# Hybrid convolution and gated linear attention block: the transposes of a token tile's scaled outputs one half-unit step later in the recurrence

## Chip, cores and metric

The kernel runs on one core of one Trainium2 chip. The metric is the device time of one execution in microseconds (us), the median of repeated runs.

## What is computed

One layer on x of shape 512 tokens x 2048. `h = rms_norm(x)`; one projection `h @ w_in` gives the inputs of two branches; their outputs side by side go through `w_out`, are added to x and normalised again. All is float32. The branch that matters here is the gated linear attention, with 4 heads, chunks of 64 tokens, and a state of 128 x 256 for each head:

```python
u = jnp.einsum('bnchk,bnchv->bnhkv', k_dec, vc)      # one update for each chunk and head
def step(state, inp):
    d, du = inp
    state = d[..., None] * state + du
    return state, state
_, s_all = lax.scan(step, init, (decay, u))
o = jnp.einsum('bnchk,bnhkv->bnchv', qc, s_all)      # every frame reads the state at its chunk's end
o = o * lax.rsqrt(jnp.mean(o * o, axis=-1, keepdims=True) + EPS) * norm_g
y_gla = o * jax.nn.silu(r)
```

The other branch is a gated short convolution over 1024 channels.

## The kernel before, in words

Tokens are held in 4 token tiles of 128 (`TT`), each of two chunks. Matrix products are made from float32r pairs: each operand is split into a rounded part (`hi`, a cast on ScalarE) and a rest (`lo`, a subtraction on VectorE), and three products hi*hi, lo*hi and hi*lo are summed in PSUM (`mm3`, lines 157 to 159).

The kernel goes through these stages. First the token-major projections (keys, values and the gate's input; tile names `tm`). Then the feature-major projections `ft`: 12 units (`ft_unit`), four for q and eight for r (`r_block`), each of 48 matmuls of 128x512 in two halves of 24. Then four Strassen-like units `st_unit` for the convolution's inputs (lines 591 to 645, tiles `pa` to `pf`, `st`, `sq`), and the output projection with its final norm (`po`, and a fifth `st_unit`).

The recurrence has no stage of its own. It is the generator `gla_steps` (line 436), and `ft_unit` calls `step()` after each half of its 24 matmuls, so the generator advances by one yield with every half unit. Step k therefore stands in the program right after half unit k, counted from 1; half units 1 to 8 belong to q, 9 to 24 to r. Where a unit ends between two steps, its tail stands between them too: for r, a multiplication on VectorE (line 493), a Silu on ScalarE (line 494) and a store to DRAM (line 495).

- Steps 1 to 6: gate, decays, and the split of token tile 0's keys and values.
- `pair_state(tt)`, steps 7, 10, 13 and 16: 24 matmuls `u` into four PSUM tiles (line 363), the state updates on VectorE (line 375), and each new state's split (`sp_hi`, `sp_lo`, lines 151 and 152).
- `chunk_splits(tt + 1)`, steps 8, 11 and 14: the split of the next tile's keys and values.
- `pair_out(tt)`, steps 9, 12, 15 and 18: 16 matmuls of q with the states into four PSUM tiles (lines 391 and 392), then the halves added (lines 394 and 395), then `out_norm`: four squares with their sums on ScalarE (line 408), a small operation on VectorE (413), a power on GpSimd (415), and four scalings of `o` by the result on ScalarE (420).
- `out_transpose(tt)`, steps 10, 13, 16 and 19 for tiles 0 to 3: eight TensorE transposes of the scaled `o` into two PSUM tiles `tp` (line 429), and eight ScalarE copies of 128x128 with the gain into `oT` (line 432). `oT` is first read much later, by `gated_rows` (line 478).

The PSUM tiles `u`, `o` and `tp` all come from one pool, `aux`, of four banks; the `ft` sums have four banks of their own. Temporaries of 128x512 come from one pool of 44 buffers (`t2`). The framework gives every engine a fixed order of instructions when the program is built: mainly the program's order, with later instructions put ahead where it expects earlier ones not to be ready. On the chip each engine works through its queue in that order.

```python
    def out_transpose(tt, o):
        for pr in range(2):
            tp = aux(f"tp{tt}_{pr}")
            for i in range(4):
                nc.tensor.transpose(out=tp[:, isl], in_=o[pr][:, isl], identity=ident)
            for i in range(4):
                nc.scalar.activation(oT[4 * pr + i][...], tp[...], AF.Copy, scale=g_v[...])
```

Of the kernel before, what the change touches and what calls it, by code (L numbers as in the profile page):

```python
# [49 lines left out]
def hybrid_block(ctx: ExitStack, tc: tile.TileContext, xT, x, params, w_tm, w_ft, w_st, w_up, b_gate, w_out, final_g, out):  # L50
# [11 lines left out]
    def t2(name):  # L62
        return k2.tile([P, S], F32, tag="k2", name=name)
# [7 lines left out]
    def aux(name):  # L71
        return ps_aux.tile([P, S], F32, tag="aux", name=name)
# [75 lines left out]
    def split_small(t, name):  # L148
        hi = t2r(f"{name}_hi")
        lo = t2r(f"{name}_lo")  # L150
        nc.scalar.copy(out=hi, in_=t)
        nc.vector.tensor_sub(out=lo, in0=t, in1=hi.bitcast(F32))
        return hi, lo
# [148 lines left out]
    def gate_transpose():  # L302
        gT = aux("gT")
        for tt in range(TT):
            nc.tensor.transpose(out=gT[0:GST, tt * P : (tt + 1) * P], in_=gst[:, tt, :], identity=ident)
        ga = t2r("ga")
        nc.vector.tensor_copy(out=ga[0:GST, :], in_=gT[0:GST, :])
        return ga

    def gate(tt, ga):  # L310
        z = aux(f"z{tt}")
        nc.tensor.matmul(z, lhsT=ga[0:GST, tt * P : (tt + 1) * P], rhs=wst, start=True, stop=True)
        e = t2(f"e{tt}")
        nc.scalar.activation(e, z, AF.Abs)
        nc.scalar.activation(e, e, AF.Exp, scale=-1.0)
        nc.scalar.activation(e, e, AF.Ln, bias=1.0)
        nc.vector.scalar_tensor_tensor(out=e, in0=z, scalar=0.0, in1=e, op0=ALU.min, op1=ALU.subtract)
        return split_small(e, f"gl{tt}")

    def gate_decay(tt, gl):  # L320
        sfx = aux(f"sfx{tt}")
        nc.tensor.matmul(sfx, lhsT=tri, rhs=gl[0], start=True, stop=False)
        nc.tensor.matmul(sfx, lhsT=tri, rhs=gl[1], start=False, stop=True)
        e = t2(f"ke{tt}")
        nc.scalar.activation(e, sfx, AF.Exp)
        for j in range(2):
            row = (j + 1) * CHUNK - 1
            nc.scalar.dma_start(out=dec8[2 * tt + j : 2 * tt + j + 1, :], in_=e[row : row + 1, :])
        nc.vector.scalar_tensor_tensor(
            out=kv[tt][0], in0=e, scalar=tail, in1=kv[tt][0], op0=ALU.max, op1=ALU.mult  # L330
        )

    def chunk_decays():
        dp = aux("dp")
        for hh in range(HEADS):
            nc.tensor.transpose(
                out=dp[:, hh * NCH : (hh + 1) * NCH], in_=dec8[0:NCH, hh * HK : (hh + 1) * HK],
                identity=ident[0:NCH, 0:NCH],
            )
        nc.vector.tensor_copy(out=decay, in_=dp[:, 0 : HEADS * NCH].rearrange("p (h c) -> p h c", c=NCH))  # L340
# [8 lines left out]
    def chunk_splits(tt):  # L349
        kv_split[tt] = [split_small(kv[tt][j], f"kv{tt}_{j}") for j in range(3)]  # L350

    def pair_state(tt):
        kp = kv_split[tt][0]
        for pr in range(2):
            vp = kv_split[tt][1 + pr]
            us = [aux(f"u{2 * tt + j}_{pr}") for j in range(2)]
            for i in range(2):
                hh = 2 * pr + i
                ksl, vsl = slice(hh * HK, (hh + 1) * HK), slice(i * HV, (i + 1) * HV)
                for k, (a, b) in enumerate(((0, 0), (0, 1), (1, 0))):  # L360
                    for j in range(2):
                        rows = slice(j * CHUNK, (j + 1) * CHUNK)
                        nc.tensor.matmul(
                            us[j][:, vsl], lhsT=kp[a][rows, ksl], rhs=vp[b][rows, vsl], start=k == 0, stop=k == 2
                        )
            for j in range(2):
                n = 2 * tt + j
                st = t2(f"s{n}_{pr}")
                if state[pr] is None:
                    nc.vector.tensor_copy(out=st, in_=us[j])  # L370
                else:
                    for i in range(2):
                        hh = 2 * pr + i
                        vsl = slice(i * HV, (i + 1) * HV)
                        nc.vector.scalar_tensor_tensor(
                            out=st[:, vsl], in0=state[pr][:, vsl], scalar=decay[:, hh, n : n + 1],
                            in1=us[j][:, vsl], op0=ALU.mult, op1=ALU.add,
                        )
                state[pr] = st
                split_state[n, pr] = split_small(st, f"sp{n}_{pr}")  # L380
# [16 lines left out]
    def pair_out(tt):  # L397
        o = [t2(f"o{tt}_{pr}") for pr in range(2)]
        for j in range(2):
            chunk_out(2 * tt + j, o)  # L400
        out_norm(tt, o)
        return o
# [19 lines left out]
    def out_transpose(tt, o):  # L422
        if not oT:
            oT.extend(t2(f"oT{b}") for b in range(8))
# [3 lines that stand above are left out]
                isl = slice(i * P, (i + 1) * P)  # L428
                nc.tensor.transpose(out=tp[:, isl], in_=o[pr][:, isl], identity=ident)
            for i in range(4):  # L430
                blk = 4 * pr + i
                nc.scalar.activation(
                    oT[blk][:, tt * P : (tt + 1) * P], tp[:, i * P : (i + 1) * P], AF.Copy, scale=g_v[:, blk : blk + 1]
                )

    def gla_steps():
        ga = gate_transpose()
        yield
        gl = []
        for tt in range(TT):  # L440
            gl.append(gate(tt, ga))
            if tt % 2:
                yield
        for tt in range(TT):
            gate_decay(tt, gl[tt])
            if tt % 2:
                yield
        chunk_decays()
        chunk_splits(0)
        yield  # L450
        done = None
        for tt in range(TT):
            pair_state(tt)
            if done is not None:
                out_transpose(tt - 1, done)
            yield
            if tt + 1 < TT:
                chunk_splits(tt + 1)
            yield
            done = pair_out(tt)  # L460
            yield
        out_transpose(TT - 1, done)

    steps = gla_steps()

    def step():
# [569 lines left out]
```

## Time and profile before

| | us |
|---|---|
| median of 3 runs | 791.43 |
| lowest and highest run | 790.61, 791.45 |
| the profiled execution, its own time | 790.9 |
| its span, first to last instruction | 788.9 |
| TensorE busy in the span | 772.4 |
| VectorE busy | 564.7 |
| ScalarE busy | 379.9 |
| GpSimd busy | 31.2 |

The profile is of one execution. Its instructions span 788.9 us, and its own time, measured as the runs are, is 790.9 us, 0.5 us under the median. Engine names in rows are PE (TensorE matmuls), PEld (its weight loads), DVE (VectorE), ACT (ScalarE), POOL (GpSimd) and SP (the queue of DMA issues). A tile is named without its number. `out<-in` says what an instruction writes and reads. In a timeline the columns are start, duration, engine, line, operation, tiles, shape and count; a bracket gives the idle time of the engine before it and what ended it. A matmul's recorded duration overlaps the next one's, so distances are taken from start to start.

### The profile page before, as it was taken

The numbers are of one execution on the slowest core, as the hardware profiler recorded it, in microseconds if no ns is written. First come the engines' busy times: TensorE is split into PE (matmuls) and PEld (weight loads), VectorE is DVE, ScalarE is ACT, GpSimd is POOL, SyncE is SP. The second block draws the span as 40 slices with busy tenths as digits, with TensorE's granted clock in tenths as the row PEclk, the third lists the DMA queues.
The fourth block names the chain that finished last, engine by engine and source line by source line (L and its number), as shares of the span: only waits on it lengthen the run. The fifth ranks groups of instructions, "written<-read, shape, count | busy, mean of one in ns | idle before, by whom it ended". The sixth has DMA issues, their size and how long they took to land. (4 is left out here: it accounts for less than half of the span.)

```text
span 788.9 us, 10098 instructions
## 1 busy us (share of the span) xinstructions
PE 772.4 (98%) x3752; PEld 663.4 (84%) x3752; DVE 564.7 (72%) x711; ACT 379.9 (48%) x574; POOL 31.2 (4%) x38
## 2 busy tenths in 40 slices
PE   9999999999999999999999999999999999999995
PEld 8999999887777878888788888888888888888885
DVE  7533242466666529998998699968987997997913
ACT  6552122364688646644544444445436344643504
POOL 1000000000000000000000000000000000003601
PEclk9999999999999999999999999999999999999998
DMA  9973334222132327877875656654655359668006
GB/s 317 324 257 88 108 121 133 88 95 76 64 107 67 103 82 260 288 219 263 297 235 187 209 179 201 211 191 164 226 186 170 127 182 364 200 195 293 24 1 213
DMA packets 48933, 140.39 MB, mean 178 GB/s; under 512 B 5827, under 2 KB 7875, under 8 KB 48885
## 3 DMA queue, kind: packets, MB, share of 16 engines
q1 hardware_dynamic: 48628, 139.74, 53.3%
q8 instruction: 29, 0.48, 0.2%
q14 instruction: 20, 0.16, 0.1%
q10 hardware_dynamic: 256, 0.02, 0.0%
HBM read 130.29 MB, written 9.44 MB: 177 GB/s over the span
## 5 line engine op out<-in xcount | busy, mean ns | idle before, releaser
L116 ACT CAST hi_sq_t<-raw_sq 128x1024 fp32r<-128x1024 f32 x80 | 84.2, 1055 | 118.5 <-PE pa L591 24.9
L117 DVE TENSOR_TENSOR lo_sq_t<-raw_sq,hi_sq_t 128x1024 fp32r<-128x1024 f32 x80 | 98.6, 1236 | 22.0 <-ACT hi_sq_t L116 21.8
L645 DVE TENSOR_TENSOR raw_sq<-raw_sq,raw_sq 128x1024 f32<-128x1024 f32 x80 | 97.0, 1219 | 5.6 <-DMA raw_sq<-in_w_st 4.7
L116 ACT CAST hi_st<-raw_st 128x1024 fp32r<-128x1024 f32 x60 | 63.2, 1054 | 68.4 <-PE pa L591 20.6
L117 DVE TENSOR_TENSOR lo_st<-raw_st,hi_st 128x1024 fp32r<-128x1024 f32 x60 | 72.1, 1220 | 13.6 <-ACT hi_st L116 13.6
L157 PE MATMUL ft<-hhi,hi_ft 128*128 128x512 f32 x192 | 75.8, 395 | 0.0
L158 PE MATMUL ft<-hlo,hi_ft 128*128 128x512 f32 x192 | 75.4, 392 | 0.0
L159 PE MATMUL ft<-hhi,lo_ft 128*128 128x512 f32 x192 | 75.2, 392 | 0.0
L117 DVE TENSOR_TENSOR lo_tm<-raw_tm,hi_tm 128x776 fp32r<-128x776 f32 x24 | 23.2, 966 | 59.1 <-ACT hi_tm L116 55.8
L262 PE MATMUL tm<-hi_tm,hhi 128*128 128x388 f32 x256 | 55.8, 339 | 0.9 <-DVE hi_tm L143 0.9
L262 PE MATMUL tm<-hi_tm,hlo 128*128 128x388 f32 x256 | 55.6, 339 | 0.0
L262 PE MATMUL tm<-lo_tm,hhi 128*128 128x388 f32 x256 | 55.4, 338 | 0.0
L116 ACT CAST hi_tm<-raw_tm 128x776 fp32r<-128x776 f32 x24 | 20.2, 842 | 68.7 <-PE tm L262 65.8
L117 DVE TENSOR_TENSOR lo_ft<-raw_ft,hi_ft 128x1024 fp32r<-128x1024 f32 x24 | 29.4, 1224 | 25.4 <-ACT hi_ft L116 25.4
L262 PEld LDWEIGHTS tm<-hi_tm,hhi 128*128 128x128 f32 x256 | 46.1, 188 | 1.1 <-ACT hhi L169 1.1
L262 PEld LDWEIGHTS tm<-lo_tm,hhi 128*128 128x128 f32 x256 | 46.0, 188 | 0.0
L262 PEld LDWEIGHTS tm<-hi_tm,hlo 128*128 128x128 f32 x256 | 45.9, 188 | 0.0
L157 PEld LDWEIGHTS ft<-hhi,hi_ft 128*128 128x128 f32 x192 | 36.1, 188 | 7.6 <-issue 0.2
L159 PEld LDWEIGHTS ft<-hhi,lo_ft 128*128 128x128 f32 x192 | 36.1, 188 | 7.6
L158 PEld LDWEIGHTS ft<-hlo,hi_ft 128*128 128x128 f32 x192 | 36.1, 188 | 7.0
L116 ACT CAST hi_ft<-raw_ft 128x1024 fp32r<-128x1024 f32 x24 | 25.2, 1050 | 31.7 <-PE ft L158 18.7
L157 PE MATMUL po<-hi_wo,yh 128*128 128x512 f32 (+1 forms) x104 | 39.6, 381 | 0.0
(279 smaller groups left out, 1642.7 us busy)
## 6 DMA issues: line engine op xcount, KB each, us to landing
raw_sq<-in_w_st SPq DMA_DIRECT2D x64, 512.0 KB, 4.1
raw_st<-in_w_st SPq DMA_DIRECT2D x48, 512.0 KB, 3.9
raw_ft<-in_w_ft SPq DMA_DIRECT2D x24, 512.0 KB, 3.5
raw_tm<-in_w_tm SPq DMA_DIRECT2D x24, 388.0 KB, 3.4
raw_sq<-in_w_out SPq DMA_DIRECT2D x16, 512.0 KB, 4.1
raw_wo<-in_w_out SPq DMA_DIRECT2D x13, 512.0 KB, 3.9
raw_st<-in_w_out SPq DMA_DIRECT2D x12, 512.0 KB, 7.5
rawx<-in_xT SPq DMA_DIRECT2D x16, 256.0 KB, 4.8
```

The costliest lines, as they stand in the source:

```text
L116: nc.scalar.copy(out=hi, in_=full)
L117: nc.vector.tensor_sub(out=lo, in0=full, in1=hi.bitcast(F32))
L157: nc.tensor.matmul(ps, lhsT=ah, rhs=bh, start=first, stop=False)
L158: nc.tensor.matmul(ps, lhsT=ah, rhs=bl, start=False, stop=False)
L159: nc.tensor.matmul(ps, lhsT=al, rhs=bh, start=False, stop=last)
L262: nc.tensor.matmul(pst[tt][:, 0:TMC], lhsT=a[:, tt * P : (tt + 1) * P], rhs=w, start=kt == 0 and k == 0, stop=kt == KT - 1 and k == 2,)
L645: nc.vector.tensor_tensor(out=dst, in0=x0, in1=x1, op=op)
```

## The change

In the loop over token tiles, `out_transpose(tt - 1, done)` stands after the yield that follows `pair_state(tt)` and no longer ahead of it, so it runs at the start of the step that also holds `chunk_splits(tt + 1)`: tiles 0, 1 and 2 in steps 11, 14 and 17 and no longer 10, 13 and 16. One more yield puts tile 3's from step 19 into step 20. No instruction is added or taken away, no size changes, and nothing of the moved part issues a DMA.

```diff
@@ -451,14 +451,15 @@
         done = None
         for tt in range(TT):
             pair_state(tt)
+            yield
             if done is not None:
                 out_transpose(tt - 1, done)
-            yield
             if tt + 1 < TT:
                 chunk_splits(tt + 1)
             yield
             done = pair_out(tt)
             yield
+        yield
         out_transpose(TT - 1, done)
 
     steps = gla_steps()
```

## Rows read from the trace of the kernel before

**Rows 1.** The profile page: its head.
```profile
span 788.9 us, 10098 instructions
```

**Rows 2.** Waits of TensorE, whole run: waiter <- releaser, us in total, times, longest.
```profile
PE tp L429 <- ACT o L420: 4.5, 4, 1.9
PE tp L429 <- ACT oT L432: 1.4, 1, 1.4
...
PE pa L591 <- DVE lo_st L117: 0.7, 1, 0.7
```

**Rows 3.** Windows: stretch, its length, busy us of each engine, clock, DMA, GB/s.
```profile
200.00:282.00 82.00, 76.03 (x420) 62.54 (x419) 49.62 (x82) 63.91 (x146) 4.04 (x4) 1.00 0.28 87
320.00:360.00 40.00, 40.00 (x178) 33.10 (x178) 40.00 (x41) 20.86 (x25) 0.00 (x0) 1.00 0.75 235
388.00:789.00 401.00, 392.98 (x1809) 327.27 (x1808) 328.09 (x362) 180.30 (x227) 23.62 (x16) 0.99 0.57 189
```

**Rows 4.** Timeline of TensorE: start, duration; a bare half unit, sixteen transposes.
```profile
281.98 0.39 PE L157 MATMUL ft<-hhi,hi_ft 128*128 128x512 f32 x1
...
287.42 0.39 PE L157 MATMUL ft<-hhi,hi_ft 128*128 128x512 f32 x1
...
624.20 0.60 PE L730 MATMUL tu<-ident,c 128*128 128x128 f32 x4
...
625.86 0.48 PE L157 MATMUL po<-hi_wo,yh 128*128 128x512 f32 x1
```

**Rows 5.** Timeline of TensorE around the transposes of token tile 0.
```profile
207.20 0.50 PE L157 MATMUL ft<-hhi,hi_ft 128*128 128x512 f32 x1
...
210.08 0.44 PE L429 MATMUL tp<-ident,o 128*128 128x128 f32 x2 [1.92 <-ACT o L420]
...
215.86 0.39 PE L157 MATMUL ft<-hhi,hi_ft 128*128 128x512 f32 x1
...
221.30 0.28 PE L391 MATMUL o<-sp_hi,qs 128*128 128x256 f32 x1
```

**Rows 6.** Timeline of TensorE around the transposes of token tile 1.
```profile
230.39 0.50 PE L157 MATMUL ft<-hhi,hi_ft 128*128 128x512 f32 x1
...
238.88 0.39 PE L157 MATMUL ft<-hhi,hi_ft 128*128 128x512 f32 x1
```

**Rows 7.** Timeline of TensorE around the transposes of token tile 2.
```profile
253.19 0.28 PE L363 MATMUL u<-kv_hi,kv_lo 64*128 64x256 f32 x2
...
257.26 0.66 PE L429 MATMUL tp<-ident,o 128*128 128x128 f32 x4 [1.43 <-ACT oT L432]
...
261.86 0.39 PE L157 MATMUL ft<-hhi,hi_ft 128*128 128x512 f32 x1
```

**Rows 8.** Timeline of TensorE: the half unit with the transposes of token tile 3 begins.
```profile
274.68 0.39 PE L157 MATMUL ft<-hhi,hi_ft 128*128 128x512 f32 x1
```

**Rows 9.** Timeline of ScalarE: start, duration, idle time before it and its releaser.
```profile
218.25 2.17 ACT L432 ACTIVATE oT<-tp,par 128x128 f32<-128x128 f32 x8
...
220.94 1.28 ACT L494 ACT_TABLE_LOAD   x1
...
228.66 1.05 ACT L116 CAST hi_ft<-raw_ft 128x1024 fp32r<-128x1024 f32 x1 [0.50 <-PE ft L158]
...
234.49 1.71 ACT L420 ACTIVATE o<-o,ro 128x256 f32<-128x256 f32 x4 [0.90 <-POOL ro L415]
...
252.88 1.71 ACT L420 ACTIVATE o<-o,ro 128x256 f32<-128x256 f32 x4 [1.32 <-POOL ro L415]
```

**Rows 10.** Timeline of VectorE: state updates, then the handover to the quarter sums.
```profile
212.38 0.87 DVE L375 SCALAR_TENSOR_TENSOR s<-s,decay,u 128x256 f32<-128x256 f32 x2
...
257.30 0.87 DVE L375 SCALAR_TENSOR_TENSOR s<-s,decay,u 128x256 f32<-128x256 f32 x2
...
293.06 0.69 DVE L493 TENSOR_TENSOR r<-ft,rB 128x512 f32<-128x512 f32 x1 [8.80 <-PE ft L159]
...
298.96 0.69 DVE L525 TENSOR_TENSOR qs<-raw_qx,raw_qx 128x512 f32<-128x512 f32 x1
```

## The prediction, made before the changed kernel ran

> **What bounds the kernel now.** I read the page's head for the span [rows 1], then TensorE's own waits over the whole run [rows 2], the windows [rows 3], and last the timelines of each stretch with a wait [rows 4 to 10]. Outside one stretch TensorE works without a pause: it is busy 40.00 of 40 us in one later window and 392.98 of 401 in the last, which holds the program's tail [rows 3]. From 200 to 282 us it is busy only 76.03 of 82 [rows 3], and the missing 6.0 us are the waits of the transposes `tp`: 4.5 us in four waits for the scaling of `o` on ScalarE, 1.4 us in one wait for the copies into `oT`, that is, for a PSUM bank [rows 2]. The rest of the run has one wait of 0.7 us for VectorE worth naming [rows 2]. So TensorE's queue sets the end, and the change moves just those instructions that make it stand still.
>
> **What each stand costs.** A half unit with nothing in it takes 5.44 us (281.98 to 287.42), and sixteen transposes in a row take 1.66 (624.20 to 625.86), so eight take about 0.85 with the return to other matmuls [rows 4]. What a half unit with transposes takes beyond 5.44 + 0.85 = 6.29 us is lost:
> - tile 0: 207.20 to 215.86 is 8.66, so 2.3 lost [rows 5];
> - tile 1: 230.39 to 238.88 is 8.49, so 2.2 lost [rows 6];
> - tile 2: its last `u` starts at 253.19, the transposes could follow 0.2 later at 253.4, and the next half unit starts at 261.86: 8.46, so 2.15 lost [rows 7];
> - tile 3: 274.68 [rows 8] to 281.98 [rows 4] is 7.30, so 0.95 lost.
>
> Together 7.6 us. It is more than the 6.0 us recorded as waits, because a matmul's recorded end lies after the point at which the next could start, and because the transposes come in lots of two and four between other matmuls.
>
> **The change part by part.** Nothing is added or removed. All 32 transposes and 32 copies move one step later, past one half unit of 24 matmuls, 5.44 us of TensorE; SP's and GpSimd's queues are not touched, since the moved code issues neither a DMA nor a GpSimd instruction. What it costs is what is late next, tile by tile.
>
> Tile 0. The transposes would be reached at 207.20 + 5.44 = 212.64, two and a half microseconds after their data came (210.08) [rows 5]. The second lot needs a second bank, which the state update on VectorE gives back at 212.38 + 0.87 = 213.25 [rows 10]; TensorE is there at 213.1. I count 0.15 lost, so 2.15 gained.
>
> Tile 1. TensorE would start the half unit at 230.39 - 2.15 = 228.24 and be at the transposes at 233.7. The four scalings run on ScalarE from 234.49 to 236.20 [rows 9], and ScalarE is busy 63.91 of the 82 us [rows 3], without a pause of note ahead of them but two: 0.50 us in which a cast waits for TensorE, and 0.90 us for the power on GpSimd [rows 9]. The first goes when TensorE is earlier, the second stays. So the last transpose can't end before about 235.9 to 236.4, where 234.55 would be free of waits: 1.3 to 1.8 lost. I take 1.5, so 0.7 gained. If tile 0 gains less, this wait shrinks by as much: ScalarE sets where TensorE stands after tile 1, at about 2.85 us ahead of now.
>
> Tile 2. TensorE arrives at 253.4 - 2.85 + 5.44 = 256.0. The scalings, 252.88 to 254.59 [rows 9], are over even if they come no earlier. The second bank is given back by the update at 257.30 + 0.87 = 258.17 now [rows 10]; its chain runs over ScalarE, earlier by at least the 0.5 us above and at most by TensorE's 2.85, so between 255.3 and 257.7, against a need at 256.5. Between no wait and 1.2 I take 0.5, so 1.65 gained. Should the bank still be the one that the first lot's copies free, the present wait of 1.43 [rows 7] is the bound.
>
> Tile 3. The transposes come 3.9 us of matmuls later than they stand now, and the wait there is at most what was lost, 0.95. I take it as gone.
>
> The copies. ScalarE makes tile 0's from 218.25, eight microseconds after the first transposes, as their place in its queue is behind the state's casts [rows 9]. So they needn't move when the transposes come at 212.6. They end at 220.42 and free the two banks that the third and fourth `o` products want; TensorE would reach the first of them at 221.30 - 2.15 = 219.15 [rows 5] and the third and fourth 1 to 1.4 us later, at 220.1 and 220.6. That fits by 0.2 us at the worst. What could be late is the unit tail that the copies now pass in the program: its Silu with a table load of 1.28 us [rows 9]. If it comes first, about 1.9 us are lost here, but TensorE then waits that much less at tile 1, so the sum is the same but for a few tenths. For later tiles I count 0.15 for such waits.
>
> The sum: 2.15 + 0.7 + 1.65 + 0.95 - 0.15 = 5.3 us. The profiled execution took 790.9 us in all, of which 788.9 are its span [rows 1]: 790.9 - 5.3 = 785.6. It was 0.5 us under the median of the runs, so I predict 786.1 us.
>
> Whether it lasts to the end: VectorE waits 8.80 us for TensorE before the quarter sums begin at 293 [rows 10], so all that follows is timed from TensorE and moves with it; nothing between there and the end is tied to a fixed time.
>
> A rule that speaks against the change: a gap that repeats on the busy engine, says the Trainium skill in "Perfetto Trace Analysis", section "Optimization Strategy", can mean that there is not enough SBUF or PSUM for the next tile. By it the sum would be about zero, since the banks would be held longer. The trace bears it out for 1.4 of the 6.0 us alone [rows 2].
>
> **The rivals.** *All waits go.* ScalarE's order changes too, and the scalings of tile 1 come before its other work. The whole 7.6 us are gained: 783.8. For it: ScalarE does work there that is not urgent, such as the scaling of later inputs. Against: nothing in the change moves that work.
>
> *The wait moves to the banks.* The copies go one half unit later on ScalarE as well: tile 0's would end at 220.42 + 5.44 = 225.9, and the fourth `o` product, due at 220.6, waits 5.3 us. TensorE is then at tile 1's transposes at 233.7 + 5.3 = 239.0 and done at 239.85, 1.0 behind now, with 1.65 + 0.95 still to gain: 1.6 gained in all, 789.8. Against: the copies already stand late in ScalarE's queue and needn't move.
>
> *Nothing moves, or nothing lasts.* Queue orders are not quite the program's: tile 0's transposes stand three matmuls inside the half unit and not ahead of it [rows 5]. They might keep their places; or what is gained is waited for again where VectorE is at 40.00 of 40 us [rows 3] and TensorE already waits 0.7 us for it [rows 2]. Time 791.4. Against: VectorE's wait of 8.80 us before that stretch [rows 10].
>
> *Slower.* VectorE has no reserve between 320 and 360 us [rows 3]. If the new order pushes the quarter sums, now begun while TensorE is still in the r units, into that stretch, TensorE pays for each at the product that waits 0.7 us now. A quarter's work takes VectorE 5.2 us (293.75 to 298.96 [rows 10]); two of them cost 10.4, so 786.1 + 10.4 = 796.5. It decides from about 6.9 us pushed, 5.3 plus the bound of no change. Against: the sums are tied to half units 21 to 24, behind everything moved.
>
> **How the numbers follow.** A measurement of this kernel can tell about 0.2%, 1.6 us, from no change. Chances: forecast 0.66, all waits go 0.09, banks 0.11, nothing 0.08, slower 0.06. The forecast alone runs from 785.1 (1.3 us lost at tile 1 and nothing elsewhere) to 788.3 (1.8 at tile 1, 1.43 at tile 2, and as much again above the count at another bank). Adding the first two rivals gives 783.8 to 789.8, which leaves out 0.14 and a margin. The bank rival lies on the bound of 0.2%, so half of it counts as faster: faster 0.66 + 0.09 + 0.05 = 0.80, same 0.08 + 0.06 = 0.14, slower 0.06.
>
> **What would show it.** In the changed profile the transposes stand behind a whole half unit of `ft` matmuls; TensorE's waits for the scaling of `o` fall from 4.5 us to 1 to 2, all at tile 1; the half units with transposes take 6.3 to 6.5 us for tiles 0 and 3, near 8 for tile 1, near 7 for tile 2; the first matmul of `pa`, right after the last `ft`, starts about 5 us earlier, and the end with it. A wait of `o` for the `oT` copies, or of `pa` for `lo_st` grown from 0.7 us, would prove me wrong, and so would transposes found at their old places.

## The result, and the profile after

The changed kernel takes **786.03 us** (median of 6 runs, 785.87 to 788.13); the kernel before, run beside it, 791.25 (6 runs, 790.61 to 792.25). The ratio is 0.9938, 95% interval 0.9925 to 0.9951. The profiled execution took 785.95 us, 783.6 of them its span. From line 463 on the changed kernel's line numbers are one higher, and an experiment's are shifted by the lines that it adds. One run of the kernel before, beside e9_state to e11_state_before, took 1343.82 us at a mean clock of 0.634 and is left out of its median there.

The head and first part of the profile page of the changed kernel, answering [rows 1]:

```profile
span 783.6 us, 10104 instructions
...
PE 773.7 (99%) x3752; PEld 664.8 (85%) x3752; DVE 563.7 (72%) x711; ACT 379.9 (48%) x574; POOL 31.6 (4%) x38
```

TensorE's waits over the whole run, answering [rows 2] (waiter <- releaser, total, times, longest):

```profile
PE warm L86 <- POOL ones L83: 1.1, 1, 1.1
PE o L391 <- ACT oT L432: 0.7, 1, 0.7
```

The first is the warm-up at the start. Of the 4.5 us for the scaling of `o`, the 1.4 us for a bank and the 0.7 us of `pa` for `lo_st`, nothing is left; one wait of `o` for the `oT` copies is new. The windows, answering [rows 3], the later two moved by about 5 us:

```profile
200.00:282.00 82.00, 81.28 (x440) 67.39 (x439) 50.93 (x84) 65.45 (x148) 4.04 (x4) 1.00 0.29 90
315.00:355.00 40.00, 40.00 (x178) 33.14 (x177) 40.00 (x40) 21.31 (x25) 0.00 (x0) 1.00 0.75 235
383.00:784.00 401.00, 392.65 (x1808) 326.96 (x1806) 327.07 (x362) 180.24 (x227) 24.02 (x16) 0.99 0.58 189
```

TensorE is busy 81.28 of 82 us where it was at 76.03. The timeline of TensorE in the changed kernel, answering [rows 5 to 8]; matmuls between the shown ones are left out:

```profile
207.09 0.50 PE L157 MATMUL ft<-hhi,hi_ft 128*128 128x512 f32 x1
...
212.66 1.24 PE L429 MATMUL tp<-ident,o 128*128 128x128 f32 x8
213.66 0.48 PE L157 MATMUL ft<-hhi,hi_ft 128*128 128x512 f32 x1
...
221.58 0.40 PE L158 MATMUL ft<-hlo,hi_ft 128*128 128x512 f32 x1
222.66 0.38 PE L391 MATMUL o<-sp_hi,qs 128*128 128x256 f32 x1 [0.69 <-ACT oT L432]
...
223.24 0.39 PE L159 MATMUL ft<-hhi,lo_ft 128*128 128x512 f32 x1
...
227.58 0.39 PE L157 MATMUL ft<-hhi,hi_ft 128*128 128x512 f32 x1
227.81 0.39 PE L158 MATMUL ft<-hlo,hi_ft 128*128 128x512 f32 x1
228.12 0.38 PE L363 MATMUL u<-kv_hi,kv_hi 64*128 64x256 f32 x1
...
229.25 0.50 PE L159 MATMUL ft<-hhi,lo_ft 128*128 128x512 f32 x1
...
230.30 0.40 PE L157 MATMUL ft<-hhi,hi_ft 128*128 128x512 f32 x1
230.72 0.35 PE L363 MATMUL u<-kv_hi,kv_hi 64*128 64x256 f32 x1
...
232.19 0.50 PE L158 MATMUL ft<-hlo,hi_ft 128*128 128x512 f32 x1
...
236.22 1.03 PE L429 MATMUL tp<-ident,o 128*128 128x128 f32 x8
237.01 0.48 PE L157 MATMUL ft<-hhi,hi_ft 128*128 128x512 f32 x1
...
251.43 0.28 PE L363 MATMUL u<-kv_hi,kv_lo 64*128 64x256 f32 x2
...
257.21 1.04 PE L429 MATMUL tp<-ident,o 128*128 128x128 f32 x8
258.01 0.48 PE L157 MATMUL ft<-hhi,hi_ft 128*128 128x512 f32 x1
...
270.94 0.39 PE L157 MATMUL ft<-hhi,hi_ft 128*128 128x512 f32 x1
...
276.38 1.04 PE L429 MATMUL tp<-ident,o 128*128 128x128 f32 x8
277.18 0.48 PE L157 MATMUL ft<-hhi,hi_ft 128*128 128x512 f32 x1
...
299.06 0.61 PE L592 MATMUL pa<-hi_st,hhi 128*128 128x512 f32 x2
```

All four sets of transposes stand in one lot of eight behind a whole half unit, and none waits. Tile 0's half unit takes 6.57 us (207.09 to 213.66), tile 3's 6.24 (270.94 to 277.18), and tile 2's stretch from 0.2 after its last `u` 6.38 (251.63 to 258.01): 0.3, none and 0.1 above the bare 6.29. Tile 1's half unit is the exception: it takes 9.43 us (227.58 to 237.01), with the 24 products `u` now inside it. What makes it so is read from ScalarE's timeline, answering [rows 9]:

```profile
211.02 0.60 ACT L151 CAST sp_hi<-s 128x512 fp32r<-128x512 f32 x1
...
217.85 0.62 ACT L151 CAST sp_hi<-s 128x512 fp32r<-128x512 f32 x1 [1.90 <-DVE s L375]
218.49 1.14 ACT L432 ACTIVATE oT<-tp,par 128x128 f32<-128x128 f32 x4
219.65 1.28 ACT L495 ACT_TABLE_LOAD   x1
220.95 0.63 ACT L495 ACTIVATE r<-r 128x512 f32<-128x512 f32 x1
221.49 1.13 ACT L432 ACTIVATE oT<-tp,par 128x128 f32<-128x128 f32 x4
...
234.53 1.71 ACT L420 ACTIVATE o<-o,ro 128x256 f32<-128x256 f32 x4 [0.81 <-POOL ro L415]
```

The Silu and its table load now stand between the two halves of tile 0's copies. The last four products `o` wait for the second half, come in a lot of their own at 222.66, and the 24 products `u` behind them come in two lots of twelve, between `ft` matmuls.

TensorE's lead on the kernel before, from the start of the same `ft` matmul in both traces (before minus changed), at the first half unit behind each tile's transposes (at tile 1 the second, half unit 16), and at the end of the span:

| kernel | tile 0 (half unit 12) | tile 1 (16) | tile 2 (18) | tile 3 (21) | end | median |
|---|---|---|---|---|---|---|
| changed | 2.20 | 1.77 | 3.86 | 4.80 | 5.29 | 786.03 |
| e1_tile0 | 2.17 | 1.02 | -1.02 | -1.06 | -0.24 | 790.75 |
| e2_tile1 | -0.99 | 1.03 | -1.86 | -1.88 | -1.14 | 792.11 |
| e3_tile2 | -1.62 | -1.62 | 0.47 | -3.68 | -3.43 | 793.94 |
| e4_tiles023 | 2.15 | 1.00 | 3.02 | 3.96 | 3.17 | 786.26 |
| e5_silu | 2.21 | 2.98 | 3.73 | 4.54 | 5.39 | 785.89 |
| e9_state | 2.59 | 4.50 | 6.58 | 7.52 | 7.99 | 782.79 |
| e11_state_before | 1.56 | 1.66 | 2.55 | 2.51 | 3.44 | 788.61 |

A lead that a trace brings along from ahead of the recurrence is in it: 0.1 us in the changed kernel, 0.5 in e2, 0.3 in e9, 0.8 in e11.

### The profile page after: what moved, and what is told of

It is laid out like the page before. It is cut to its first block, busy times and chain, and to the rows that moved or that the text cites. A ratio compares the mean times of both kernels' runs of the same rounds, so it can differ in the third digit from the quotient of the medians.

```text
span 783.6 us, 10104 instructions
## 1 busy us (share of the span) xinstructions
PE 773.7 (99%) x3752; PEld 664.8 (85%) x3752; DVE 563.7 (72%) x711; ACT 379.9 (48%) x574; POOL 31.6 (4%) x38
## 4 chain that ended last, share of the span: by engine, by line
PE 96%; ACT 1%; DVE 1%; issue 1%; POOL 0%; ACTq 0%; POOLq 0%
PE tm L262 17%; PE pa L592 14%; PE pc L592 7%; PE pb L592 7%; PE pf L592 7%; PE pe L592 7%; PE pd L592 7%; PE ft L159 5%; PE ft L157 5%; PE ft L158 5%; PE po L159 3%; PE po L158 3%; PE po L157 3%; PE u L363 1%; PE warm L86 1%
## 5 line engine op out<-in xcount | busy, mean ns | idle before, releaser
L851 POOL TENSOR_TENSOR res<-res,fg 128x512 f32<-128x512 f32 x12 | 21.8, 1850 | 449.0 <-DMA fg<-in_final_g 443.0
```

The costliest lines, as they stand in the source:

```text
L851: nc.gpsimd.tensor_mul(out=res[tt][cbk], in0=res[tt][cbk], in1=fg[cbk])
```

## Experiments: one tile at a time

The first four kernels choose for each tile which place its transposes have. All of them run the changed kernel's code with

```diff
             pair_state(tt)
+            if done is not None and tt - 1 not in LATE:
+                out_transpose(tt - 1, done)
             yield
-            if done is not None:
+            if done is not None and tt - 1 in LATE:
                 out_transpose(tt - 1, done)
...
-        yield
+        if TT - 1 in LATE:
+            yield
         out_transpose(TT - 1, done)
```

**e1_tile0**, `LATE = (0,)`:

> Only token tile 0's transposes come one step later; tiles 1 to 3 stay where the kernel before has them. Theory A (the order set by ScalarE: once tile 0 is moved, the Silu with its table load of 1.28 us cuts its oT copies in two, the o products and the next u come in two lots each, and TensorE can't pass tile 1 before ScalarE's scalings end near 236.2 us): 2.1 us gained at tile 0, some of it given back by tile 1, 1.6 to 2.1 gained in all, about 789.4 us. Tile 1's transposes still wait for the scaling, though not longer than before. Theory B (each tile by itself): 2.1 gained at tile 0 and nothing lost at tile 1, because the loss there comes from moving tile 1: 789.1 us, with the half unit of tile 1 at 8.5 us as before.

Measured: 790.75 us (789.84 to 791.22), ratio 1.0001 (0.999 to 1.0011). Tile 0's gain is all there, 2.1 us, and so are the wait of `o` for `oT`, 0.7 us, and the loss up to tile 1. They need tile 0's move alone. At tile 2 the transposes, in their early place, wait 2.0 us for the scaling, only 0.2 more than the two waits of the kernel before there (0.34 and 1.43). The rest of the 2.05 us lost there (1.02 to -1.03) goes where TensorE's clock falls behind that wait (0.57 granted from 256 to 260 us); the clock comes below. Both theories' times, 789.4 and 789.1, are missed.

**e2_tile1**, `LATE = (1,)`:

> Only token tile 1's transposes come one step later. Theory A: the o products and u of tile 1's stretch stay in one lot (the cut copies come from tile 0's move), TensorE reaches the transposes at 230.4 + 5.4 = 235.8 us, within 0.5 us of the last scaling (236.2), so 1.6 to 2.0 us of the 2.2 lost there are gained: about 789.5 us. Theory B (tile 1's move is what costs in the changed kernel, whose half units 13 and 14 took 0.95 us longer than before): 0.9 us slower, 792.2 us.

Measured: 792.11 us (791.04 to 793.33), ratio 1.0019 (1.0005 to 1.0033). That is theory B's number, but not its mechanism: tile 1's own move brings 2.0 us of lead (-0.99 to 1.03), as A had it. The time is lost elsewhere. At tile 0, where the program is that of the kernel before, the clock falls (0.68 granted from 208 to 212 us) and the lead goes from 0.5 to -0.99. Tile 2's early transposes wait 3.08 us, 1.3 more than before, and the clock falls again (0.65 from 256 to 260).

**e3_tile2**, `LATE = (2,)`:

> Only token tile 2's transposes come one step later. Both theories: 1.65 to 2.15 us gained at tile 2, no new wait behind it; about 789.2 us. If instead the second lot waits for a bank (the bound in the prediction), 0.7 to 1.0 is gained and TensorE shows a wait of the transposes for the state update or the oT copies.

Measured: 793.94 us (793.8 to 794.55), ratio 1.0045 (1.0029 to 1.0062): slower. Tile 2's move brings 2.1 us (-1.62 to 0.47), and tile 3's early transposes wait 3.14 us for their scaling where they waited 0.64. The other part of the loss is the clock, which comes below.

**e4_tiles023**, tile 1 put back, `LATE = (0, 2, 3)`:

> The changed kernel with token tile 1 alone put back to its old step; tiles 0, 2 and 3 stay late. Theory A: ScalarE's scalings set where TensorE leaves tile 1 either way, so the time is the changed kernel's within 0.4 us, 785.8 to 786.5, and tile 1's transposes show a wait for the scaling of 0.3 to 1.0 us. Theory B: 0.95 us faster than the changed kernel, 785.1 us. If moving tile 1 does help on top of tile 0: 1 to 2 us slower than the changed kernel, 787 to 788.

Measured: 786.26 us (785.8 to 787.86), ratio 0.995 (0.9932 to 0.9968); its profiled execution is the slowest of these, with a wait of 1.3 us of `pa` for `lo_st`. Tile 1's transposes wait 0.3 us for the scaling, and the time is in theory A's range. Moving tile 1 on top of the others is worth 0.2 us between medians, and 0.8 of lead in the traces (4.80 against 3.96 at tile 3).

What follows from the four: the cut of the copies and the wait of `o` come from tile 0's move, as theory A has it, and putting tile 1 back gains nothing, against theory B. And the gains don't add. In e2_tile1 and e3_tile2 the next transposes that still stand early wait 1.3 and 2.5 us longer than in the kernel before, where 2.0 and 2.1 had just been won, and all three traces lose another 1.5 to 1.8 us at each fall of the clock. Of the three tiles moved alone none made the kernel faster; tile 3 alone wasn't tried. How much the waits without the falls would have taken isn't shown.

## Experiments: what held tile 1, and what came after it

**e5_silu** takes the table load out of the copies, with a small Silu in step 6:

```diff
         chunk_decays()
         chunk_splits(0)
+        warm = small.tile([P, 1], F32, tag="warm", name="warm", bufs=1)
+        nc.scalar.activation(warm, decay[:, 0, 0:1], AF.Silu)
         yield
```

> The changed kernel, with one small Silu of 128x1 in step 6, so that ScalarE loads Silu's table there and not between tile 0's two lots of oT copies. In the program built, the 16 products o then stand in one lot and the 24 products u of tile 2 too, as in the kernel before. Theory A (the table load of 1.28 us and the lots that it cuts are what tile 1 lost): the wait of 0.7 us of o for oT is gone, tile 1's half unit falls from 9.4 us to 7.5 to 8.5, its scalings end about 1.3 us earlier, and the time falls from 786.0 to 784.3 to 785.2 us. Rival B (ScalarE's floor at tile 1 is set by GpSimd's power and the other casts, the table load lies beside them): o waits less, the transposes of tile 1 wait as much more, 785.7 to 786.3.

Measured: 785.89 us (785.48 to 786.32), ratio 0.9934 (0.9922 to 0.9945), no faster than the changed kernel by more than 0.2 us. Locally theory A held: `u` comes in one lot, and the lead behind tile 1 is 2.98 and not 1.77. No transposes of tile 1 wait. Of `o`'s wait for `oT` it was wrong, which stays at 0.72 us; and tile 2 took the gain back. TensorE, VectorE and ScalarE of e5_silu at tile 2, from three timelines:

```profile
257.75 0.63 PE L429 MATMUL tp<-ident,o 128*128 128x128 f32 x4 [1.14 <-DVE s L375]
```

```profile
256.74 0.86 DVE L375 SCALAR_TENSOR_TENSOR s<-s,decay,u 128x256 f32<-128x256 f32 x2
```

```profile
252.31 1.71 ACT L420 ACTIVATE o<-o,ro 128x256 f32<-128x256 f32 x4 [1.32 <-POOL ro L415]
253.92 1.03 ACT L116 CAST hi_ft<-raw_ft 128x1024 fp32r<-128x1024 f32 x1
254.86 0.61 ACT L151 CAST sp_hi<-s 128x512 fp32r<-128x512 f32 x1
```

The second lot of transposes wants the bank that the state update at 256.74 gives back. Read backwards: that update stands on VectorE behind the rest of the state's split, which needs the cast at 254.86, which stands on ScalarE behind the scalings at 252.31, which had waited 1.32 us for GpSimd's `ro`. The chain of the states, then, queues behind the scalings and waits for a power it doesn't need. At tile 0 it is the same: in the changed kernel the first `sp_hi` starts at 211.02, right behind the scalings, and all later casts, and `oT`'s copies behind them, are late by that.

**e7_silu_qx1** is e5_silu and also queues the scalings of `raw_qx` behind tile 1's scalings of `o`:

```diff
+AFTER = 1
...
-                nc.scalar.activation(o[pr][:, vsl], o[pr][:, vsl], AF.Copy, scale=ro[:, hh : hh + 1])
+                scaled[tt] = nc.scalar.activation(o[pr][:, vsl], o[pr][:, vsl], AF.Copy, scale=ro[:, hh : hh + 1])
...
-                nc.scalar.activation(raw[:, sl], raw[:, sl], AF.Copy, scale=g_in[:, k0 + i : k0 + i + 1])
+                with tc.issue_after(scaled[AFTER].ins):
+                    nc.scalar.activation(raw[:, sl], raw[:, sl], AF.Copy, scale=g_in[:, k0 + i : k0 + i + 1])
```

> As e5_silu, and the scalings of raw_qx on ScalarE, not urgent here, are ordered behind the four scalings of tile 1's o. Theory A (every us of other work ahead of tile 1's scalings on ScalarE is paid by TensorE): tile 1's half unit reaches 6.3 to 7 us, no wait of the transposes is left, and the time is 783.3 to 784.3 us, the 783.8 of the first rival in the prediction. Rival B (ScalarE has room ahead of the scalings once the table is loaded): as e5_silu within 0.3 us, and with the quarter sums starting later, perhaps a longer wait of pa for lo_st, up to 787.

Measured: 786.29 us (785.82 to 786.56), ratio 0.9939 (0.9927 to 0.995). Tile 1's scalings start 1.9 us earlier than in e5_silu (231.79 against 233.68), so the order did change. The wait at tile 2 is 1.15 us as in e5_silu, and more room ahead of tile 1 is worth nothing. Theory A fell.

**e6_two** moves the transposes one step further, ahead of `pair_out`:

```diff
             pair_state(tt)
             yield
-            if done is not None:
-                out_transpose(tt - 1, done)
             if tt + 1 < TT:
                 chunk_splits(tt + 1)
             yield
+            if done is not None:
+                out_transpose(tt - 1, done)
             done = pair_out(tt)
             yield
         yield
+        yield
         out_transpose(TT - 1, done)
```

> The transposes two half-unit steps later than in the kernel before, just ahead of the products o of the next tile, which want the same four banks. Theory A (the banks are the next limit; one step is as late as it pays): the third and fourth product o of tiles 1, 2 and 3 come behind copies of 1.1 us each and more ScalarE work; o waits for oT appear, 1 to 3 us in all, and part of the gain is lost: 787 to 790 us. Rival B (the later the better: tile 1's floor falls away, since its scalings are long done): no transposes wait, tile 1's 3.1 us lost come back, 783 to 785 us.

Measured: 787.02 us (786.72 to 787.93), ratio 0.995 (0.9937 to 0.9963). No transpose waits; `o` waits for `oT` three times, 1.4 us in all. By the medians one step is the better place by 1.0 us, though the two intervals overlap; theory A holds at the low end of its range.

**e9_state** gives the states their turn first. It is the changed kernel with the scalings of tiles 0 to 2 issued behind the next tile's first cast:

```diff
-        nc.scalar.copy(out=hi, in_=t)
+        last_cast[:] = [nc.scalar.copy(out=hi, in_=t)]
...
                 split_state[n, pr] = split_small(st, f"sp{n}_{pr}")
+                while pending:
+                    with tc.issue_after(last_cast[0].ins):
+                        out_scale(*pending.pop())
...
         nc.gpsimd.tensor_tensor(out=ro, in0=ms, in1=nhalf, op=ALU.pow)
+        if tt == TT - 1:
+            out_scale(o, ro)
+        else:
+            pending.append((o, ro))
```

where `out_scale` holds the four scalings unchanged.

> The changed kernel, with the four scalings of o of tiles 0 to 2 queued on ScalarE behind the first cast sp_hi of the next tile's states; until now ScalarE stood 1.3 to 2 us idle for GpSimd's ro ahead of the scalings while that cast's data were there. Theory A (the chain of the states, cast, rest, update, runs behind the scalings, and sets when banks come free and when oT's copies start): the first sp_hi of tiles 0 and 2 starts 1.5 to 3 us earlier, the scalings no more than 0.3 later, the wait of o for oT of 0.7 us shrinks or goes, and the time falls from 786.0 to 784.3 to 785.4. Rival B (the table load and the scalings alone set TensorE's place after tiles 0 and 1): no more than 0.3 us gained, 785.6 to 786.3.

Measured: **782.79 us** (782.33 to 783.57), ratio 0.9893 (0.9878 to 0.9908), better than theory A asked. It beats both kernels. ScalarE's timeline of e9_state:

```profile
208.51 0.62 ACT L153 CAST sp_hi<-s 128x512 fp32r<-128x512 f32 x1 [0.66 <-DVE s L377]
209.22 1.71 ACT L433 ACTIVATE o<-o,ro 128x256 f32<-128x256 f32 x4
...
215.79 1.14 ACT L445 ACTIVATE oT<-tp,par 128x128 f32<-128x128 f32 x4
216.95 1.28 ACT L508 ACT_TABLE_LOAD   x1
...
232.19 1.71 ACT L433 ACTIVATE o<-o,ro 128x256 f32<-128x256 f32 x4 [0.90 <-POOL ro L420]
...
252.43 0.62 ACT L153 CAST sp_hi<-s 128x512 fp32r<-128x512 f32 x1 [2.07 <-DVE s L377]
252.96 1.71 ACT L433 ACTIVATE o<-o,ro 128x256 f32<-128x256 f32 x4
```

The first cast fits into the time in which ScalarE stood idle; it starts 2.5 us earlier than in the changed kernel (208.51 against 211.02), and the scalings follow without a wait. `oT`'s copies start 2.7 us earlier (215.79 against 218.49), so the table load between them no longer delays `o`; tile 1's scalings come 2.3 us earlier (232.19 against 234.53). TensorE's waits and the window of e9_state show what is left:

```profile
PE warm L86 <- POOL ones L83: 1.1, 1, 1.1
```

```profile
200.00:282.00 82.00, 82.00 (x451) 68.83 (x450) 50.88 (x84) 65.91 (x148) 4.05 (x4) 1.00 0.31 95
```

82.00 of 82 us: TensorE has no pause there any more.

**e10_silu_state** is e5_silu with e9_state's order.

> The kernel of e5_silu with the order of e9_state. In e5_silu tile 1's wait went, and in its place came a wait of 1.14 us of tile 2's transposes for the state update that gives a bank back, and one of 0.72 of o for oT. Theory A (both stand behind the scalings that wait for ro): both waits go, and the time falls from 785.9 to 783.0 to 784.2 us, near the 783.8 at which no wait is left. Rival B (the bank is late for another reason, VectorE's other work or the late u): the wait at tile 2 stays over 0.8 us and the time 785.5 to 786.2.

Measured: 782.96 us (782.79 to 783.34), ratio 0.9895 (0.9881 to 0.9909): the same as e9_state, at the edge of theory A's range. Both of e5_silu's waits are gone, as theory A has it, and the early table load is worth nothing by itself.

**e11_state_before** is the kernel before with e9_state's order alone.

> The kernel before, with the order of e9_state alone: the transposes stay where they were. Theory A (there the transposes wait for the scalings, which wait for ro, and a quicker chain of the states doesn't help; only the wait of 1.43 us for oT at tile 2 can go): the waits for the scaling of o stay at 4 to 5.5 us, 789.3 to 791.3 us. Rival B (the order on ScalarE was the fault and the place of the transposes is not needed): waits under 2 us in all, 785 to 787.

Measured: 788.61 us (787.44 to 789.2), ratio 0.9967 (0.9955 to 0.998). Its waits:

```profile
PE tp L442 <- ACT o L433: 4.1, 4, 1.7
```

The four waits for the scaling are still there, as theory A said; the wait for a bank is gone. The time is 0.7 us under A's range, for a reason that isn't shown; its trace, of the fastest of the six runs, is 0.8 us ahead before the recurrence moves anything. The order alone brings 2.8 us (791.42, the median of the kernel before there, to 788.61), the move alone 5.2, both 8.6 (791.42 to 782.79): each removes what the other can't.

## Experiment: the clock

In e3_tile2 TensorE's granted clock falls to half in two stretches. Windows of e3_tile2, whose 0.83 and 0.84 are means over 10 and 11 us, and under them the first stretch in the kernel before:

```profile
207.00:217.00 10.00, 8.10 (x36) 6.25 (x33) 5.64 (x12) 4.56 (x12) 1.02 (x1) 0.83 0.15 52
...
276.00:287.00 11.00, 8.94 (x36) 7.36 (x37) 2.37 (x4) 7.71 (x19) 1.01 (x1) 0.84 0.22 69
```

```profile
207.00:217.00 10.00, 8.08 (x44) 6.34 (x40) 5.63 (x12) 5.48 (x13) 1.02 (x1) 1.00 0.18 54
```

TensorE's timeline of e3_tile2 at the first of them:

```profile
210.10 0.44 PE L430 MATMUL tp<-ident,o 128*128 128x128 f32 x2 [1.90 <-ACT o L421]
...
212.03 0.63 PE L158 MATMUL ft<-hhi,hi_ft 128*128 128x512 f32 x1
212.46 0.63 PE L159 MATMUL ft<-hlo,hi_ft 128*128 128x512 f32 x1
```

Behind the wait of 1.90 us the matmuls stand 0.43 us apart and not 0.227 (5.44 over 24), the step of the lower of the clock's two levels, 1.2 GHz. It costs 1.6 us, the lead that e3_tile2 loses at tile 0, where its program is that of the kernel before. **e8_fill** is e3_tile2 with useless transposes of the identity in the waits:

```diff
+FILL = {0: 16, 1: 16, 3: 28}
...
             tp = aux(f"tp{tt}_{pr}")
+            for _ in range(FILL.get(tt, 0) if pr == 0 else 0):
+                nc.tensor.transpose(out=tp[:, 0:P], in_=ident[...], identity=ident[...])
```

> The kernel of e3_tile2 (793.94 us, TensorE's clock at half in two stretches after waits of 1.9 and 3.1 us) with useless transposes of the identity ahead of the real ones, 16 at tiles 0 and 1 and 28 at tile 3, so that TensorE works where it stood still. Theory A (the clock falls after such a wait): the extra transposes take 1.66, 1.66 and 2.9 us, inside the waits; no stretch at half clock between 200 and 290 us, and what the two stretches cost, 1.6 us each, comes back: 790.3 to 791.3 us. Rival B (the clock falls for another reason, whatever TensorE does there): two stretches at half clock again and 793.5 to 794.5. Rival C (the extra transposes come too late to fill the wait and add to it): 795 to 799.

Measured: 796.22 us (794.43 to 797.5), ratio 1.0067 (1.0055 to 1.008). Windows of e8_fill:

```profile
207.00:217.00 10.00, 8.10 (x47) 6.70 (x47) 5.47 (x13) 3.91 (x10) 1.02 (x1) 1.00 0.16 52
...
276.00:287.00 11.00, 10.56 (x62) 8.62 (x60) 2.09 (x3) 8.21 (x22) 1.01 (x1) 1.00 0.22 72
```

The clock stays at 1.00 in both stretches, and its mean over an execution is 0.996 to 0.998 in all six runs, against 0.992 or 0.993 in all five of e3_tile2. So far theory A holds. The time doesn't: the transposes, extra and real, wait 2.6 us in all for the state updates that give banks back, and the extra ones come partly behind the data they were to bridge, as rival C has it. That the clock costs 1.6 us a fall rests on e3_tile2's trace, not on this time.

## Why the prediction was right, and where not

786.1 us were predicted, 786.03 measured, and the lead at the end of the span is 5.29 us against 5.3. The main mechanism held: the transposes moved past a half unit and none waits for the scaling any more. That the sum agrees to the tenth is luck. The recurrence gave 4.7 us (2.1 - 0.43 + 2.1 + 0.94 at the four tiles), 0.6 less than counted, and a wait outside the sum, of `pa`, happened to be missing and made it up. The prediction had also named a wait of `o` for the `oT` copies as a sign that would prove it wrong, and that wait is there, 0.69 us.

**Tile 0** (2.15 predicted): 2.1 gained; the half unit is 6.57 us, 0.3 above bare, where 0.15 was put down for the bank. (From the prediction's own rows tiles 0 and 3 lost 2.37 and 1.01 us, not 2.3 and 0.95: 7.75 in all and not 7.6.)

**Tile 1** (0.7 predicted) and the copies (0.15 set aside) are the steps that failed. The prediction expected TensorE to be at the transposes at 233.7 and to lose 1.5 us waiting for the scalings. The scalings do end where it put them, 236.24, but TensorE doesn't wait: it comes there at 236.22, having lost the time earlier. The prediction had named the cause, the Silu with its load ahead of part of the copies, and argued that what `o` loses the transposes get back. They waited for nothing, and the sum still fell short, since the `u` behind `o` came in split lots. The kernel before has its 24 `u` in pairs, from

```profile
228.78 0.38 PE L363 MATMUL u<-kv_hi,kv_hi 64*128 64x256 f32 x2
```

to 230.39 [rows 6], 1.70 us from where the next `ft` was due, 228.69. In the changed kernel the two lots, counted in the same way, take 1.21 (228.04 to 229.25) and 1.66 (230.53 to 232.19): 1.17 more. The last four `o` put 1.43 us between two `ft` matmuls (1.66 from 221.58 to 223.24, less a step of 0.23) where four of the kernel before's one lot of sixteen take 0.48: about 0.95 more. Some 0.3 us lie in slower steps of `ft` right behind the lots. Against these 2.4 us stand 2.0 that the transposes of tile 1, in one lot and without a wait, take less than before. The lead went from 2.20 to 1.77 over tile 1 where the prediction had 2.15 to 2.85: 1.1 us short. That the split lots are worth this is shown by e5_silu: there `o` waits as long (0.72 us), `u` comes in one lot, and the lead is 1.2 us more (2.98). The floor that the prediction put under tile 1, the end of the scalings, was not what held TensorE in the changed kernel or in e5_silu; it shows only in e4_tiles023, as a wait of 0.3 us. What held it was ScalarE's order ahead of it, which the prediction took as fixed: e9_state, which changes it, brings the lead there to 4.50, 2.7 more, of which 0.2 is brought along from ahead of the recurrence.

**Tile 2** (1.65): 2.1 gained (1.77 to 3.86); the bank's wait, put at 0.5 between 0 and 1.2, is nil. With TensorE 1.2 us earlier it is 1.14 (e5_silu), so the range was right, and the value hung on where tile 1 left TensorE. **Tile 3** (0.95): 0.94 (3.86 to 4.80).

**Not in the sum.** `pa`'s wait of 0.7 us for `lo_st` [rows 2] is gone in this profile, and the lead grows by 0.65 behind `pa`'s first matmul (4.68 to 5.33 at the first `po`). That is not the change's sure gain: the wait is 0.7 in the profile of before, 0 in that of after, 0.4 in e3_tile2, 1.3 in e4_tiles023. What decides it stays open.

**The rivals.** Nothing moved to the banks but 0.7 us. The Trainium skill's rule in "Perfetto Trace Analysis", section "Optimization Strategy", that a repeating gap can mean too little PSUM, was taken to speak against the change. It bears on the smaller part here: waits for a bank were 1.4 of the 6.0 us before and are the new 0.7 now, and the other 4.5 us went with the same four banks. "All waits go" put 7.6 us on the recurrence; e9_state comes near with 7.1 (7.99 us of lead, of which 0.3 was brought along and 0.6 came behind `pa`'s first matmul). Slower was not seen here, but e3_tile2 shows that it was within reach of a quarter of the change, by a mechanism that no rival had.

## What to carry to other kernels

Measure a wait from what it waits for, not from its length: here ScalarE's order set when the data came and when banks came free, and moving TensorE's work at one tile alone brought nothing that lasted (790.75, 792.11 and 793.94 us), while three tiles without tile 1 brought nearly all (786.26). When an instruction on an in-order engine waits for a third engine, look what stands behind it that is ready; putting one cast ahead of such a wait was worth 3.2 us on top of the move (786.03 to 782.79). Count how a group of small matmuls splits when one of them is delayed, not only the delay.

## What was not expected of the hardware

**The clock.** TensorE's granted clock fell to half behind some waits of 1.9 to 3.1 us: once in the trace of e1_tile0 and twice in those of e2_tile1 and e3_tile2. It didn't fall behind the wait of 1.92 us in the profile of before [rows 5], at the same place. The Trainium skill, "TensorE: Matmul & The Clock Gate", section "What's actually happening", puts an idle TensorE at 1.2 GHz and a busy one at 2.4; the steps of 0.43 and 0.227 us agree.

Whether part of the gain in the medians is the clock's stays open. The 5.29 us between the two traces are not: in neither does the clock fall from 200 to 282 us (1.00 in both [rows 3]). In the job of the first four experiments the runs of the kernel before with a mean clock of 0.997 or 0.998 took 789.07 to 789.88 us but for one of 791.36, and those at 0.996 or less 790.87 to 793.22, as if some had a fall. But in the two later jobs the groups overlap (789.99 to 790.84 and one of 792.73, against 790.32 to 792.83). And the one execution of before that was traced, 790.9 us at 0.996, has no fall behind a wait; its clock is low only at the end, where TensorE has no work left (0.50 from 784 to 788 us). A mean of 0.996 is thus no sign of a fall.

**Two small matmuls at once.** Two `u` products that read 64 rows each start together in the kernel before (x2), by its program one for each chunk, and the 24 take 1.70 us. In the first lot of the changed kernel most starts still come in pairs, one product apart, and twelve take 1.21 us. In the second the first six start one after the other from 230.72, five of them before the first of the other six at 231.31, and twelve take 1.66 us.
